# Gates of half the tokens by indirect transfers through a matrix in DRAM, in a four-layer decoder with product-key experts

## The chip, the cores and the metric

One core of one Trainium2 chip runs the whole program in one launch. The metric is the device time of an execution in microseconds (us), lower being better. TensorE is the engine of the matrix products (PE, its weight loads PEld), VectorE is DVE, ScalarE is ACT, GpSimd is POOL; SyncE (SP) issues most DMA transfers.

## The reference

256 tokens of width 1024 go through four layers. Each has a token mixer (sliding-window, dilated, latent, sliding-window), a normalisation, the product-key expert stage `peer`, and a second normalisation. `peer` takes most of the time:

```python
q = (t @ w_q).reshape(n_tok, 8, 2, 128)
sc = einsum('thpd,hpkd->thpk', q, keys)            # 8 heads x 2 halves x 128 keys
s_top, i_top = top_k(sc, 16)
cand = s_top[:, :, 0, :, None] + s_top[:, :, 1, None, :]
best, sel = top_k(cand.reshape(n_tok, 8, 256), 16) # 16 experts of 16384 for a head
idx  = (i_top[..0..] * 128 + i_top[..1..]) at sel
gate = softmax(best)
h = gelu(einsum('cd,ced->ce', t, u[idx]))          # 128 experts for a token
y = einsum('ce,ced->cd', gate * h, v[idx])
```

All data are float32. An expert that two heads of one token pick gets the sum of both gates.

## The kernel before, in words

The kernel gathers no rows of `u` and `v`. It multiplies all 256 tokens with all 16384 experts and zeroes what is not chosen: `G[expert, token] = gelu(t u) * gate`, and `y = G v`, where the gate is 0 for experts not chosen. A float32 product is made of three products of float32r parts (hi*hi, lo*hi, hi*lo): ACT makes `hi`, DVE or POOL makes `lo = raw - hi` (`_split`, L82).

All weights come as one list of 512 KB chunks (`plan`, L49), in the order of use. `nxt` (L98) hands out a chunk: it splits up to two chunks ahead (`SPLITAHEAD`), and SP loads up to three ahead of the splits (`RAWBUFS`). Every engine's order is the order of the Python calls.

`peer` (L892) has these stages for each layer:

- **Scores** (`peer_scores`, L720): 16 chunks of `w_q`, then products with the keys.
- **First products** (the loop over j at L928, 128 chunks of `u`): 24 matmuls of 256 columns (L121) give the scores of 128 experts for 256 tokens, ACT applies Gelu into `G`. `G[0]` holds the first 64 chunks, `G[1]` the rest.
- **Second products** (the loop at L969, 128 chunks of `v`): ACT and DVE split `G[j]` (L961, L962), and 12 matmuls of 512 columns (L131 to L135) add to `y`. The last five chunks go through `sum_norm`.

Under the first products a side generator runs on DVE, paced by a budget of estimated DVE microseconds for each chunk (`pace`, L708; each `yield` names a cost). It is first `topk_gen` (L744): the 16 best of 128 scores for each half of each head and both halves of the tokens, candidates, 16 best of those, their row and column among 128x128 experts, softmax; TensorE turns the table (L855). Then it is `weights_gen` (L859): for each unit of 4 tokens DVE builds two one-hot matrices (L869, L871; one carries the gate), and TensorE multiplies them into a 128x128 gate matrix for each token (L885), 64 units in all. `keep` (L904) brings that into `G`: for chunks whose Gelu comes later it is copied by ACT, and Gelu is multiplied in (`times`, L923); for chunks already there DVE multiplies (L917). `pool_share` says which part of the `lo` subtractions POOL takes.

## Time and profile before

| what | value |
|---|---|
| median of 3 runs | 3997.86 us (3997.18 to 3999.26) |
| profiled execution, own time | 4000.66 us |
| profiled execution, span on the core | 3998.8 us |
| TensorE busy | 98% of the span |
| VectorE, ScalarE, GpSimd busy | 75%, 47%, 8% |
| bytes moved | 668.00 MB, 167 GB/s in the mean |

The span runs from the first to the last instruction; the profiled execution's own time has 1.9 us more around it. Busy time is the union of an engine's instructions; since matmuls are pipelined, the distance from start to start tells more of their price than their duration.

### The profile page before, as it was taken

The numbers are of one execution on the slowest core, as the hardware profiler recorded it, in microseconds if no ns is written. First come the engines' busy times: TensorE is split into PE (matmuls) and PEld (weight loads), VectorE is DVE, ScalarE is ACT, GpSimd is POOL, SyncE is SP. The second block draws the span as 40 slices with busy tenths as digits, with TensorE's granted clock in tenths as the row PEclk, the third lists the DMA queues.
The fourth block names the chain that finished last, engine by engine and source line by source line (L and its number), as shares of the span: only waits on it lengthen the run. The fifth ranks groups of instructions, "written<-read, shape, count | busy, mean of one in ns | idle before, by whom it ended". The sixth has DMA issues, their size and how long they took to land. (4 is left out here: it accounts for less than half of the span.)

```text
span 3998.8 us, 68740 instructions
## 1 busy us (share of the span) xinstructions
PE 3934.8 (98%) x26592; PEld 3579.7 (90%) x26592; DVE 3017.9 (75%) x5798; ACT 1894.6 (47%) x3568; POOL 336.1 (8%) x135
## 2 busy tenths in 40 slices
PE   8999999999999999999999999999999999999999
PEld 6999998888998999988887999998888899998887
DVE  7888985566667989965557888985566788996555
ACT  5444444445554444444445444434445444444444
POOL 0111110000001111100000111110000111110000
PEclk9999999999999999999999999999999999999999
DMA  5454445564444554455653554445564455445554
GB/s 182 161 185 151 143 148 187 203 215 156 140 143 143 175 174 143 138 169 189 215 182 105 169 183 152 143 142 187 197 221 148 143 181 168 143 138 175 189 199 159
DMA packets 188007, 668.00 MB, mean 167 GB/s; under 512 B 20688, under 2 KB 27408, under 8 KB 187168
## 3 DMA queue, kind: packets, MB, share of 16 engines
q1 hardware_dynamic: 187424, 663.46, 49.8%
q8 instruction: 209, 3.42, 0.3%
q14 instruction: 118, 0.97, 0.1%
q0 software_dynamic: 64, 0.08, 0.0%
q10 hardware_dynamic: 192, 0.07, 0.0%
HBM read 662.46 MB, written 1.07 MB: 166 GB/s over the span
## 5 line engine op out<-in xcount | busy, mean ns | idle before, releaser
L94 DVE TENSOR_TENSOR lo<-raw,hi 128x1024 fp32r<-128x1024 f32 x1083 | 1324.3, 1223 | 825.4 <-ACT hi L88 821.7
L88 ACT ACTIVATE hi<-raw 128x1024 fp32r<-128x1024 f32 x1212 | 1281.3, 1058 | 724.6 <-PE y L135 696.3
L121 PE MATMUL hp<-zh,hi 128*128 128x256 f32 x5360 | 784.5, 289 | 2.5 <-ACT zh L222 1.7
L121 PE MATMUL hp<-zh,lo 128*128 128x256 f32 x5360 | 752.6, 283 | 0.0
L121 PE MATMUL hp<-zl,hi 128*128 128x256 f32 x5360 | 751.3, 283 | 0.0
L121 PEld LDWEIGHTS hp<-zh,hi 128*128 128x128 f32 x5360 | 689.4, 192 | 9.6 <-issue 4.5
L121 PEld LDWEIGHTS hp<-zh,lo 128*128 128x128 f32 x5360 | 691.7, 192 | 0.0
L121 PEld LDWEIGHTS hp<-zl,hi 128*128 128x128 f32 x5360 | 691.4, 192 | 0.0
L133 PE MATMUL y<-lo,wk 128*128 128x512 f32 x2004 | 632.5, 396 | 0.0
L131 PE MATMUL y<-hi,wk 128*128 128x512 f32 x2004 | 629.0, 394 | 3.5 <-ACT wk L961 3.3
L135 PE MATMUL y<-hi,wk 128*128 128x512 f32 x2004 | 631.8, 396 | 0.2 <-DVE wk L999 0.2
L94 POOL TENSOR_TENSOR lo<-raw,hi 128x1024 fp32r<-128x1024 f32 (+1 forms) x129 | 334.7, 2596 | 3293.6 <-ACT hi L88 3090.5
L131 PEld LDWEIGHTS y<-hi,wk 128*128 128x128 f32 x2004 | 375.7, 188 | 96.6 <-ACT wk L961 4.1
L135 PEld LDWEIGHTS y<-hi,wk 128*128 128x128 f32 x2004 | 376.0, 188 | 93.3 <-DVE wk L999 0.6
L133 PEld LDWEIGHTS y<-lo,wk 128*128 128x128 f32 x2004 | 376.2, 188 | 89.2
L941 ACT ACTIVATE gtmp<-hp 128x256 f32<-128x256 f32 (+52 forms) x284 | 80.6, 284 | 615.3 <-PE hp L121 313.6
L869 DVE TENSOR_TENSOR wk<-iota,tab 128x1024 f32<-128x1024 f32 x256 | 314.1, 1227 | 0.1
L885 PE MATMUL y<-wk 128*128 128x128 f32 x2048 | 271.1, 275 | 13.5 <-DVE wk L871 13.5
L885 PEld LDWEIGHTS y<-wk 128*128 128x128 f32 x2048 | 250.2, 192 | 15.7 <-DVE wk L871 15.7
L871 DVE TENSOR_TENSOR wk<-wk,tab 128x512 f32<-128x512 f32 x256 | 245.7, 960 | 8.8
L946 ACT ACTIVATE G<-hp 128x256 f32<-128x256 f32 x228 | 87.6, 384 | 340.9 <-PE hp L121 340.6
L962 DVE TENSOR_TENSOR wk<-G,wk 128x256 fp32r<-128x256 f32 x492 | 206.0, 419 | 2.4 <-ACT wk L961 2.4
(190 smaller groups left out, 2686.0 us busy)
## 6 DMA issues: line engine op xcount, KB each, us to landing
raw<-in_peer_u SPq DMA_DIRECT2D x512, 512.0 KB, 3.3
raw<-in_peer_v SPq DMA_DIRECT2D x512, 512.0 KB, 3.3
raw<-in_dil_w SPq DMA_DIRECT2D x72, 512.0 KB, 3.6
raw<-in_peer_wq SPq DMA_DIRECT2D x64, 512.0 KB, 3.6
raw<-in_swa_w SPq DMA_DIRECT2D x20, 512.0 KB, 4.0
G<-in_lnp SPq DMA_DIRECT2D x16, 512.0 KB, 4.6
raw<-in_swa_wo SPq DMA_DIRECT2D x16, 512.0 KB, 3.5
G<-relb SPq DMA_DIRECT2D x12, 512.0 KB, 4.7
```

Of the source, the lines that this page charges most:

```text
L88: nc.scalar.activation(h[:, :w], r[:, :w], AF.Copy)
L94: eng.tensor_sub(lo[:, :w], r[:, :w], h.bitcast(F32)[:, :w])
L121: mm(ps, w[:, k, :], z[:, k0 + k, :], start=(p == 0 and k == 0), stop=(p == 2 and k == nk - 1))
L131: mm(ps[t][b][:, :s.stop - s.start], zh[:, ts], hi[:, s], start=first, stop=False)
L133: mm(ps[t][b][:, :s.stop - s.start], zh[:, ts], lo[:, s], start=False, stop=False)
L135: mm(ps[t][b][:, :s.stop - s.start], zl[:, ts], hi[:, s], start=False, stop=last)
L869: V.tensor_tensor(ab, self.iota[:, None, None, :].to_broadcast(shape), tab[:, 0:2, ts][:, :, :, None].to_broadcast(shape), op=OP.is_equal)
L871: V.tensor_mul(ab[:, 1], ab[:, 1], tab[:, 2, ts][:, :, None].to_broadcast([128, 4, 128]))
L885: nc.tensor.matmul(p[:, k, :], ab[:, 0, k, :], ab[:, 1, k, :], start=True, stop=True)
L941: nc.scalar.activation(tmp[:, 0:td], ps[:, 0:td], AF.Gelu)
L946: nc.scalar.activation(g, ps, AF.Gelu)
L962: nc.vector.tensor_sub(gz[:, 1, :], g, gz.bitcast(F32)[:, 0, :])
```

## The change

The 256 tokens are treated in two halves.

- For tokens 0 to 127 no matrices are built by TensorE. A matrix of 128x128x128 floats (8 MB) in DRAM, `gates[i]`, one for each layer, is zeroed beforehand by 64 transfers of 128 KB on SP's queue (`next_gates`, `clear`). `topk_gen` now finishes this half of the tokens first, makes an element number for each of a token's 128 experts (`ids`, column * 16384 + row * 128 + token), and calls `ready`. That issues 128 indirect transfers on POOL's queue (`scatter`): each adds one float for each of the 128 tokens. The 16 transfers of a head may be in flight together; each head waits until the head before it has landed.
- In the second products, `gated(j)` multiplies `G[j]`'s first 128 columns by the gates, which SP fetches two chunks at a time (128 KB) into two buffers `gt`. The first fetch waits for all transfers of `scatter`.
- For tokens 128 to 255 everything stays, with 32 units in place of 64, from the last token down.
- The costs in the `yield`s and the budgets are changed (2.0 for a chunk until the first half is ready, then 1.6; before 1.3). POOL takes 40% of the `lo` subtractions until `ready` and none after it (before 20%). POOL's queue isn't tied to the program's order against the other engines any more.

```diff
+    def clear(self, n):
+        while n and self.to_clear:
+            n -= 1
+            self.nc.sync.dma_start(self.to_clear.pop(0), self.zero[:, None, :].to_broadcast([128, 2, 128]))
+    def next_gates(self, i):
+        self.clear(999)
+        self.gates.append(self.dram.tile([128 * 128 * 128, 1], F32, name=f"gates{i}"))
+        v = self.gates[-1].rearrange("(n p b c) o -> n p b (c o)", p=128, b=2, c=128)
+        self.to_clear = [v[k] for k in range(64)]
     def nxt(self, ahead=SPLITAHEAD):
         i = self.n_use
+        self.clear_acc += self.clear_rate
+        while self.clear_acc >= 1:
+            self.clear_acc -= 1
+            self.clear(1)
...
-            self.pace(1.3)
+            self.pace(2.0)
...
+            if t == 0:
+                V.tensor_scalar(row, row, 128.0, self.steps[:, 32:33], op0=OP.mult, op1=OP.add)
+                yield 0.28
+                V.scalar_tensor_tensor(col, col, 16384.0, row, op0=OP.mult, op1=OP.add)
+                yield 0.28
+                V.tensor_copy(ids, col)
+                yield 0.28
...
+            if t == 0:
+                ready()
...
-        for u in range(66):
-            if u + 1 < 64:
+        for u in range(34):
+            if u + 1 < 32:
                 build(u + 1)
...
+    def scatter(self, i, ids, val):
...
+        for h in range(8):
+            head = f"gates {i} {h}"
+            new = []
+            for k in range(16 * h, 16 * h + 16):
+                ins = self.nc.gpsimd.indirect_dma_start(
+                    self.gates[i], IndirectOffsetOnAxis(ap=ids[:, k:k + 1], axis=0), val[:, k:k + 1], None,
+                    compute_op=OP.add).ins
+                if new:
+                    tc.declare_no_dep(ins, group=head, reason="experts of one head differ")
+                self.all_done(ins, sent, "the same token's gates of another head")
...
+        def ready():
+            self.clear(999)
+            self.pool_share = 0.0
+            sent.extend(self.scatter(i, ids, val))
+
+        self.side = self.topk_gen(ids, val, tab, ready)
+        self.pool_share = 0.4
...
-                rate = 67.0 / (125 - j)
+                rate = 35.0 / (125 - j)
+            if j == 64 and i + 1 in self.layers:
+                self.next_gates(i + 1)
+                self.clear_rate = 0.5
...
+        rows = self.gates[i].rearrange("(n b p c) o -> n p b (c o)", b=2, p=128, c=128)
+        gts = []
+        def fetch(n):
+            while len(gts) < min(n, 64):
+                gt = self.misc.tile([128, 2, 128], F32, name="gt", bufs=2)
+                ins = nc.sync.dma_start(gt, rows[len(gts)]).ins
+                if not gts:
+                    self.all_done(ins, sent, "the gates are read")
+                gts.append(gt)
+        def gated(j):
+            if j < 128:
+                fetch(j // 2 + 2)
+                g = G[j // 64][:, j % 64, 0:128]
+                nc.vector.tensor_mul(g, g, gts[j // 2][:, j % 2, :])
...
         n = 128 - YTAIL
+        gated(0)
+        gated(1)
         z = split_g(0)
         for j in range(n):
+            gated(j + 2)
             hi, lo = self.nxt(min(SPLITAHEAD, n - 1 - j))
...
+            self.next_gates(self.layers[0])
+            self.clear_rate = 2.0
```

Three places of the order, all in the first layer. In the rows of the changed kernel, `L97` is the `lo` subtraction, `L81` the load of a chunk, `L929` the indirect transfer, `L1027` the fetch, `L1036` the multiplication by fetched gates, `L105` a clearing transfer, `L987` is `times`, `L1042` the split of `G`; names in brackets are what the instruction waits for (`DMAHW` and `DMASW` are transfers of SP's and of POOL's queue).

First, POOL's queue under the first products. Before, it holds only `lo` subtractions there. Now, after the 16th of them:

```order
L97 TENSOR_TENSOR lo<-raw,hi 128x1024 [waits DMAHW5_49,PE_49,Activation_49]
L929 DMA gates_140<-gt 2097152x1 [waits DMAHW7_49,DMAHW2_49,DVE_49]
L929 DMA gates_140<-gt 2097152x1 x5
L929 DMA gates_140<-gt 2097152x1 [waits DMASW0_49]
...
L929 DMA gates_140<-gt 2097152x1 [waits DMASW1_49]
L929 DMA gates_140<-gt 2097152x1 [waits DMASW4_49,DMASW5_49,DMASW3_49,DMASW6_49,DMASW2_49,DMASW7_49,DMASW1_49,DMASW0_49]
L929 DMA gates_140<-gt 2097152x1 x7
L929 DMA gates_140<-gt 2097152x1 [waits DMASW2_49]
```

Within a head's 16 transfers the later ones wait, one after another, for transfers issued eight before them; the first of the next head waits for all eight lanes. No subtraction stands among the 128 transfers.

Second, SP's queue at the change from first to second products. Before:

```order
L78 DMA raw<-in_peer_u 128x1024 [waits DMAHW5_49,DVE_49]
L78 DMA raw<-in_peer_v 128x1024 [waits DMAHW6_49,Pool_49]
L78 DMA raw<-in_peer_v 128x1024 [waits DMAHW7_49,DVE_49]
L78 DMA raw<-in_peer_v 128x1024 [waits DMAHW0_49,DVE_49]
L78 DMA raw<-in_peer_v 128x1024 [waits DMAHW1_49,DVE_49]
```

Now:

```order
L81 DMA raw<-in_peer_v 128x1024 [waits DMAHW6_49,DVE_49]
L81 DMA raw<-in_peer_v 128x1024 [waits DMAHW4_49,DMAHW0_49,DVE_49]
L1027 DMA gt<-gates_140 128x2x128 [waits DMASW4_49,DMASW5_49,DMASW3_49,DMASW6_49,DMASW2_49,DMASW7_49,DMASW1_49,DMASW0_49]
L1027 DMA gt<-gates_140 128x2x128
L1027 DMA gt<-gates_140 128x2x128 [waits DMAHW7_49,DMAHW5_49,DVE_49]
L105 DMA gates_4232<-zero 256x1x128
L81 DMA raw<-in_peer_v 128x1024 [waits DMAHW1_49,DVE_49]
```

The first fetch stands behind the load of the fifth chunk of `v`, waits for POOL's transfers, and all further loads stand behind it.

Third, DVE at the same place. Before:

```order
L94 TENSOR_TENSOR lo<-raw,hi 128x1024 [waits DVE_49,DMAHW2_49,PE_49,Activation_49]
L924 TENSOR_TENSOR G_3644<-G_3644,gtmp 128x256
L924 TENSOR_TENSOR G_3644<-G_3644,gtmp 128x256 [waits Activation_49]
L962 TENSOR_TENSOR wk<-G_1675,wk 128x256 [waits DVE_49,Activation_49]
L94 TENSOR_TENSOR lo<-raw,hi 128x1024 [waits DVE_49,DMAHW3_49,PE_49,Activation_49]
L962 TENSOR_TENSOR wk<-G_1675,wk 128x256 [waits Activation_49]
```

Now:

```order
L97 TENSOR_TENSOR lo<-raw,hi 128x1024 [waits DVE_49,DMAHW0_49,PE_49,Activation_49]
L987 TENSOR_TENSOR G_4003<-G_4003,gtmp 128x128
L987 TENSOR_TENSOR G_4003<-G_4003,gtmp 128x128 [waits Activation_49]
L1036 TENSOR_TENSOR G_1724<-G_1724,gt 128x128 [waits DMAHW5_49]
L1036 TENSOR_TENSOR G_1724<-G_1724,gt 128x128
L1042 TENSOR_TENSOR wk<-G_1724,wk 128x256 [waits Activation_49]
L1036 TENSOR_TENSOR G_1724<-G_1724,gt 128x128 [waits DMAHW6_49]
L97 TENSOR_TENSOR lo<-raw,hi 128x1024 [waits DMAHW1_49,PE_49,Activation_49]
```

A multiplication that waits for a fetch now stands ahead of each split of `G` and each `lo`. Counted along the queues, `ready` follows the 56th `lo` subtraction (40 on DVE and 16 on POOL); the subtractions run two chunks ahead of the products, and 34 chunks lie before the first products, so that is at chunk 19 of the 128.

## Rows read from the trace of the kernel before

**Rows 1.** The page's part 1: engine, busy us (share of the span), instructions.
```profile
PE 3934.8 (98%) x26592; PEld 3579.7 (90%) x26592; DVE 3017.9 (75%) x5798; ACT 1894.6 (47%) x3568; POOL 336.1 (8%) x135
```
**Rows 2.** Busy time of each engine in stretches of the first layer: the mixer, first products with the side generator on top-k, first products with units, second products, and the change to the next layer. Last: granted clock, share of the DMA engines, GB/s.
```profile
10.00:95.00 85.00, 76.30 (x535) 63.51 (x534) 69.82 (x203) 46.52 (x125) 4.88 (x2) 1.00 0.49 162
153.00:310.00 157.00, 157.00 (x1311) 157.00 (x1311) 132.99 (x377) 77.64 (x114) 28.68 (x11) 1.00 0.54 181
310.00:583.00 273.00, 269.75 (x2283) 269.14 (x2281) 259.18 (x380) 114.38 (x288) 37.52 (x14) 1.00 0.43 144
583.00:942.00 359.00, 358.93 (x1540) 288.80 (x1541) 217.39 (x277) 175.42 (x257) 0.39 (x1) 1.00 0.58 198
946.00:950.00 4.00, 3.02 (x19) 3.05 (x20) 3.38 (x5) 0.97 (x2) 0.28 (x1) 0.78 0.66 230
```
**Rows 3.** Timeline of PE, first products without units (start us, duration us): the first matmuls of one chunk and of the next (a chunk is three such groups of 8; the second row is cut by the window's end).
```profile
302.79 1.12 PE L121 MATMUL hp<-zh,hi 128*128 128x256 f32 x8
305.67 0.40 PE L121 MATMUL hp<-zh,hi 128*128 128x256 f32 x2
```
**Rows 4.** The same with units: a unit (four float32 matmuls, eight instructions) and the next one; one chunk lies between them (the last row is cut by the window's end).
```profile
318.71 1.05 PE L885 MATMUL y<-wk 128*128 128x128 f32 x8
322.48 0.38 PE L885 MATMUL y<-wk 128*128 128x128 f32 x2
```
**Rows 5.** Timeline of PE: the turning of the top-k table.
```profile
308.55 0.82 PE L855 MATMUL sm<-ident,G 128*128 128x128 f32 x6
```
**Rows 6.** The page's part 5: units on PE, the one-hot matrices and the `lo` subtraction on DVE (busy us, mean ns | idle before); and from the waits of PE: what units waited for (us in total, times, longest).
```profile
L885 PE MATMUL y<-wk 128*128 128x128 f32 x2048 | 271.1, 275 | 13.5 <-DVE wk L871 13.5
L869 DVE TENSOR_TENSOR wk<-iota,tab 128x1024 f32<-128x1024 f32 x256 | 314.1, 1227 | 0.1
L871 DVE TENSOR_TENSOR wk<-wk,tab 128x512 f32<-128x512 f32 x256 | 245.7, 960 | 8.8
L94 DVE TENSOR_TENSOR lo<-raw,hi 128x1024 fp32r<-128x1024 f32 x1083 | 1324.3, 1223 | 825.4 <-ACT hi L88 821.7
PE y L885 <- DVE wk L871: 13.5, 11, 1.7
```
**Rows 7.** DVE under the first products: two first instructions of one top-16 of 128 scores and of the next, with one `lo` subtraction between them (timeline); and the group of 128x128 float32 multiply-like instructions (by line, 150 to 310 us).
```profile
181.28 0.27 DVE L760 MAX8 G<-G 128x8 f32<-128x128 f32 x1
183.99 0.28 DVE L760 MAX8 G<-G 128x8 f32<-128x128 f32 x1
L823 DVE TENSOR_TENSOR G<-G 128x128 f32<-128x128 f32 x2 | 0.6, 292 | 0.1
```
**Rows 8.** POOL: its only transfers of 128 pieces are two plain loads, one shown (duration ns min/median/max); its `lo` subtractions; one of them in the timeline, and a conversion on DVE beside it.
```profile
L1098 POOL DMA_DIRECT2D iota<-in_iota x1: 540/540/540, 1.9 to 1.9; - x1
L94 POOL TENSOR_TENSOR lo<-raw,hi x129: 1807/2410/3402, 90.1 to 3628.3; 128x1024 fp32r<-128x1024 f32 x127, 128x768 fp32r<-128x768 f32 x2
192.13 3.18 POOL L94 TENSOR_TENSOR lo<-raw,hi 128x1024 fp32r<-128x1024 f32 x1 [11.99 <-ACT hi L88]
193.95 1.51 DVE L778 CAST G<-G 128x256 f32<-128x256 uint32 x1
```
**Rows 9.** DMA issues: what, queue, count, KB each, median us from issue to landing. A chunk comes in 128 pieces of 4 KB, `relb` in 512 pieces of 1 KB; `y` is written to DRAM.
```profile
raw<-in_peer_v SPq DMA_DIRECT2D x512, 512.0 KB, 3.3
G<-relb SPq DMA_DIRECT2D x12, 512.0 KB, 4.7
y<-x SPq DMA_DIRECT2D x4, 256.0 KB, 2.0
iota<-in_iota POOLq DMA_DIRECT2D x1, 64.0 KB, 5.2
```
**Rows 10.** The page's part 3: SP's queue: packets, MB, share of 16 engines' span.
```profile
q1 hardware_dynamic: 187424, 663.46, 49.8%
```
**Rows 11.** The change from first to second products in the first layer: DVE's `lo` of the chunk two ahead, the loads SP issues behind it (three, merged), PE's last group and its first of the second products, DVE's split of `G`.
```profile
580.82 1.23 DVE L94 TENSOR_TENSOR lo<-raw,hi 128x1024 fp32r<-128x1024 f32 x1 [1.32 <-ACT hi L88]
582.07 6.83 SPq L78 DMA_DIRECT2D raw<-in_peer_v  x3
581.12 1.12 PE L121 MATMUL hp<-zl,hi 128*128 128x256 f32 x8
583.07 0.73 PE L131 MATMUL y<-hi,wk 128*128 128x512 f32 x2 [0.83 <-ACT wk L961]
583.09 0.42 DVE L962 TENSOR_TENSOR wk<-G,wk 128x256 fp32r<-128x256 f32 x1
```
**Rows 12.** Timeline of PE at the change of layers: an idle time, and the matmuls after it.
```profile
946.98 2.61 PE L217 MATMUL sm<-gtmp,x 128*128 128x128 f32 x16 [2.57 <-DVE x L180]
949.24 2.25 PE L121 MATMUL hp<-zh,hi 128*128 128x256 f32 x8
951.29 1.28 PE L121 MATMUL hp<-zh,lo 128*128 128x256 f32 x8
```
**Rows 13.** Timeline of DVE in the second products: `lo`, split of `G`, the next `lo`.
```profile
702.07 1.23 DVE L94 TENSOR_TENSOR lo<-raw,hi 128x1024 fp32r<-128x1024 f32 x1 [1.24 <-ACT hi L88]
703.21 0.42 DVE L962 TENSOR_TENSOR wk<-G,wk 128x256 fp32r<-128x256 f32 x1
704.87 1.23 DVE L94 TENSOR_TENSOR lo<-raw,hi 128x1024 fp32r<-128x1024 f32 x1 [1.24 <-ACT hi L88]
```

More of the change, by code (lines that the diff above doesn't have):

```diff
@@ L8 @@
 from concourse import mybir
+from concourse.bass import IndirectOffsetOnAxis
 from concourse.bass_utils import run_bass_kernel_spmd
@@ L39 @@
 YTAIL = 5
+ET = mybir.EngineType
+ORDERED = {ET.PE, ET.DVE, ET.Activation, ET.SP}
 class Kernel:
@@ L837, in topk_gen @@
-        V.tensor_copy(den[:, 0, :][:, :, None], b3[:, :, 0:1])
-        V.tensor_sub(b3, b3, den[:, 0, :][:, :, None].to_broadcast([128, 16, 16]))
-        yield 0.2
-        nc.scalar.activation(best, best, AF.Exp)
-        yield 0.2
-        V.tensor_reduce(den[:, 1, :], b3, axis=AX.X, op=OP.add)
-        yield 0.2
-        V.reciprocal(den[:, 2, :], den[:, 1, :])
-        yield 0.2
-        for t in range(2):
-            V.tensor_mul(stk[:, t, 2, :].rearrange("p (h k) -> p h k", h=8), best[:, t],
-                         den[:, 2, 8 * t:8 * t + 8][:, :, None].to_broadcast([128, 8, 16]))
-            yield 0.2
+                yield 0.7
@@ new lines, in topk_gen @@
+                V.tensor_reduce(col[:, ks].rearrange("p (h k) -> p h k", h=4), ohb, axis=AX.X, op=OP.add)
+                yield 1.23
+            V.tensor_copy(row, idi[:, 1, :])
+            yield 0.28
+            if t == 0:
+                V.tensor_scalar(row, row, 128.0, self.steps[:, 32:33], op0=OP.mult, op1=OP.add)
+                yield 0.28
+                V.scalar_tensor_tensor(col, col, 16384.0, row, op0=OP.mult, op1=OP.add)
+                yield 0.28
+                V.tensor_copy(ids, col)
+                yield 0.28
@@ new lines, in topk_gen @@
+            V.tensor_copy(den[:, 0, :][:, :, None], best[:, :, 0:1])
+            V.tensor_sub(best, best, den[:, 0, :][:, :, None].to_broadcast([128, 8, 16]))
+            yield 0.5
+            nc.scalar.activation(best, best, AF.Exp)
+            yield 0.2
+            V.tensor_reduce(den[:, 1, :], best, axis=AX.X, op=OP.add)
+            yield 0.28
+            V.reciprocal(den[:, 2, :], den[:, 1, :])
+            yield 0.2
+            V.tensor_mul((stk[:, 2, :] if t else val).rearrange("p (h k) -> p h k", h=8), best,
+                         den[:, 2, :][:, :, None].to_broadcast([128, 8, 16]))
@@ L850, in topk_gen @@
+            yield 0.28
+            if t == 0:
+                ready()
         yield 0
         yield 0
-        for t in range(2):
-            p = self.small((128, 4, 128))
-            for q in range(3):
-                nc.tensor.transpose(p[:, q, :], stk[:, t, q, :], self.ident)
-            V.tensor_copy(tab[:, 0:3, t * 128:t * 128 + 128], p[:, 0:3, :])
-            yield 0.2
+        p = self.small((128, 4, 128))
+        for q in range(3):
+            nc.tensor.transpose(p[:, q, :], stk[:, q, :], self.ident)
@@ L859, in weights_gen @@
+        V.tensor_copy(tab, p[:, 0:3, :])
+        yield 0.55
     def weights_gen(self, tab, keep):
@@ L887, in weights_gen, with all_done @@
                 due()
-            due = keep(4 * u - 4, kept.rearrange("p t j -> p j t")) if kept is not None else None
+            due = keep(256 - 4 * u, kept.rearrange("p t j -> p j t")) if kept is not None else None
             kept = p
             yield 1
+    def scatter(self, i, ids, val):
+        tc = self.tc
+        sent = []
+        for h in range(8):
[8 more added lines that the diff above has]
+                self.all_done(ins, sent, "the same token's gates of another head")
+                tc.add_to_no_dep_group(head, ins)
+                new.append(ins)
+            sent = new
+        return sent
+    def all_done(self, ins, sent, reason):
+        for old in sent:
+            self.tc.add_manual_dep(ins, old.name, mybir.DependencyInfo(
+                mybir.DependencyClass.Sync, mybir.DependencyReason.DATA), reason=reason)
     def peer(self, i, turn):
@@ L996, in peer @@
                 gh, gl = [self.misc.tile([128, 1, T], F32R, name="gtmp", bufs=2) for _ in range(2)]
+            for q in range(m if k else 0):
+                gated(n + k + q)
             g = G[1][:, 64 - YTAIL + k:64 - YTAIL + k + m, :]
```

113 lines of the change are left out of this document (54 added, 59 removed).

## The prediction, made before the changed kernel ran

> **What bounds the kernel now.** I read the page's shares first: TensorE is busy for 98% of the span, VectorE for 75%, GpSimd for 8% [rows 1]. Then the stretches of one layer: under the first products TensorE is busy for 157.00 of 157 us and, with units, 269.75 of 273; in the second products for 358.93 of 359, and the granted clock is 1.00 (2.4 GHz) in all three [rows 2]. So every stage of `peer` ends with TensorE, and only what shortens its list shortens the time, as long as nothing else becomes later than it. The engine to watch is DVE: with units it is busy for 259.18 of 273 us [rows 2]. The DMA engines are at 0.43 to 0.58.
>
> **What is removed from TensorE.** A chunk of first products without a unit takes 305.67 - 302.79 = 2.88 us [rows 3]; with one unit, from unit to unit, 322.48 - 318.71 = 3.77 us [rows 4]. A unit so costs 0.89 us. (Its group in the page says 271.1 us for 256 units [rows 6]; that union of pipelined spans is 1.06 each, and the start-to-start distance is what the path gives back.) 32 units fewer in 4 layers are 128 x 0.89 = 113.9 us. Three of the six turns of the table go too, half of 0.82 us [rows 5], in 4 layers 1.6 us. Together **-115.5**.
>
> Units waited 13.5 us for their one-hot matrices [rows 6]. DVE then has one unit (1227 + 960 ns [rows 6]) for about every second chunk instead of for every one; I take back 5 us of the 13.5, since waits at the first units can stay; ends 0 and 13.5.
>
> **What stays hidden on DVE.** Each of 128 chunks needs one `lo` of 1.22 us [rows 6], which POOL takes no part of after `ready`. Top-k for the second half has a budget of 1.6 for a chunk. A top-16 of 128 scores takes 183.99 - 181.28 = 2.71 us with one `lo` among it [rows 7], so about 1.5 without, and the new `yield`s count 1.77 for it: a budget of 1.6 is about 1.4 us of work. 1.4 + 1.22 = 2.6 of 2.88 us: below TensorE, with a tenth to spare. With units at about 0.5 for a chunk DVE has 1.1 + 1.22 and some 0.5 for the multiplications into `G`, 2.8 of 3.3 us. In the second products it has 1.23 + 0.42 us for each 2.80 us [rows 13] and gets a 128x128 multiplication of 0.29 [rows 7]: 1.94. All this costs nothing.
>
> **The scatter.** It has from chunk 19 of the first products to their end: 108 chunks x 2.88 + 32 units x 0.89 = 340 us. It needs 8 heads x (16 c + L), where c is POOL's time for one indirect transfer and L the landing of a head's last. No row shows an indirect transfer. Low ends: the plain POOL load of 128 pieces, 0.54 us [rows 8], and the landing of the only larger DRAM write, 2.0 us [rows 9]: 8 x (8.6 + 2.0) = 85 us. High ends: the longest POOL instruction that reads SBUF beside a busy DVE, 3.40 us [rows 8], and POOL's own landing, 5.2 us [rows 9]: 8 x (54.4 + 5.2) = 477 us, 137 us late in each layer. I take c = 1.2, about twice the plain load, because that row is the nearest (POOL writes 128 pieces in both, and here also reads 128 numbers and asks for an addition), and L = 3.3: 8 x (19.2 + 3.3) = **180 us of 340**, so it costs nothing. It becomes late from c = 2.45.
>
> The DMA engines must carry it too: 16384 pieces of 4 bytes for each layer, 1024 for an engine. With about half of 340 us free [rows 2], a piece may hold an engine for 170/1024 = 0.17 us. A mean packet of 3.5 KB holds one for 0.498 x 16 x 3998.8/187424 = 0.17 us [rows 10], and I take a piece of 4 bytes to be cheaper.
>
> **Clearing and fetching.** 64 + 64 transfers of 128 KB for each layer, in 256 pieces of 512 bytes. 512 KB in 512 pieces land in 4.7 us against 3.3 in 128 pieces [rows 9]; 24 more pieces on each engine for 1.4 us, at most 0.058 us a piece, so a transfer of 256 pieces takes at most 0.93 us of the engines. By bytes alone it would be a quarter of a chunk's, under 0.5. In the second products a fetch comes every two chunks, in their first half a clearing transfer too: at most 0.17 + 0.17 on top of 0.58 [rows 2]. That is 0.92, still under 1. A fetch is issued behind the load that follows one `lo`, and its data are wanted two chunks and a split later, 2 x 2.80 + 0.42 = 6.0 us; it lands after 3.3 to 4.7 us. So in the steady state it costs nothing. In the first layer's mixer two clearing transfers stand ahead of each load; the engines are at 0.49 there [rows 2], TensorE is idle for 9 of 85 us already, and I add 3 us (0 to 15).
>
> **The new wait.** At the change to the second products the first fetch stands on SP behind the load that waits for DVE's `lo`: 582.07 in this trace [rows 11]. Issued 0.33 us later and landing after 3.3 us plus some 0.5 behind a full chunk, it is there at 586.2. Then `gated(0)` (0.29 us), ACT's split (about 0.4) and the handovers: TensorE starts at 587.1 instead of 583.07 [rows 11], 4.0 us later. Behind that wait on SP stand the next loads, and on DVE the split of `G` and the next `lo`; two further chunks are split already, so nobody but TensorE feels it. An idle time of 2.57 us was followed by eight matmuls in 2.05 us that otherwise take 0.96, and the granted clock is 0.78 in that stretch [rows 2, 12]; I add 1.5 us for it. 5.5 us x 4 = **+22**. With landings of 2.0 and 5.2 us the ends are +9 and +29.
>
> One more Exp for each layer (and its table) goes to ACT, busy for 114 of 273 us [rows 2]: nothing.
>
> **Sum.** -115.5 - 5 + 22 + 3 = -95.5 us, from the profiled execution's 4000.66 to 3905.2. That execution stands 2.8 us above the median of the runs, so **3902 us** is my time. The ends of the unknown terms make its own range 3875 to 3924.
>
> **The rivals.**
> - *The scatter comes late, and the kernel is slower.* POOL's queue becomes the bound: SP's first fetch waits for the last head, and all loads of `v` stand behind it, four times in a run. For it: a POOL subtraction of median 2.41 us took 3.18 while DVE ran a conversion, which took 1.51 us itself [rows 8], and DVE is over 90% busy; waiting for landings of earlier transfers adds to c. Against it: 0.54 us for the plain load. It decides from c = 2.64 on, where 8 x (42.2 + 3.3) = 364 us is 24 us late in each layer and the gain is gone. At c = 3.4 it is 137 us late: +548 - 95 gives some 4450; at c = 2.9 and L = 4, 403 us, 63 late, 4154. The Trainium skill, *SBUF — State Buffer*, section "A bandwidth-pool intuition that's wrong (but worth ruling out)", says that a transfer prepared by GpSimd that takes about 620 ns alone takes about 3100 beside a VectorE copy, because GpSimd can't write its descriptors while VectorE holds the shared port; with that figure the chain would be an estimated 423 us and the time 4234. The trace agrees as far as the two stretched instructions go, but most of DVE's work after `ready` isn't copies.
> - *Late by less than the gain* (c of 2.45 to 2.64, or pieces that hold the engines for about 0.17 us): 3902 to 3990.
> - *The gain is eaten elsewhere.* If DVE's instructions wait for POOL's, half a transfer (0.6 us) for each `lo`, DVE needs 3.2 of 2.88 us for the 62 chunks of the scatter: 0.35 x 62 x 4 = 87 us, 3989. Or pieces of 512 bytes cost 0.1 us and not 0.058: the first half of the second products needs 0.58 + 2 x 0.29 = 1.16 of the engines, 64 x 2.8 x 0.16 x 3 layers = 86 us, 3988. Both together with the other slips end within 0.2% of before.
> - *The change doesn't do what it says*, for instance because POOL's order puts subtractions among the transfers: in the order none stands there, so I give it nothing.
>
> **How the numbers follow.** Forecast 0.62, partly late 0.07, eaten elsewhere 0.08 (0.05 of it within 0.2%), late and slower 0.23. What a measurement of this kernel can tell from no change is about 0.2%, 8 us. Faster: 0.62 + 0.07 + 0.03 = 0.72; the same 0.05; slower 0.23. The range begins at the forecast's low end, 3875, and reaches up over the eaten gains into the smaller lateness, to 4090 (c of about 2.8); some 0.06 lies below it and 0.14 above.
>
> **What would show it.** Right: 1024 unit matmuls on PE at the same spacing; POOL's 128 transfers start at chunk 19 and end about 180 us later, well ahead of the second products; PE idle for about 5 us at each change to them; raised DMA shares of at most 0.9. Wrong: PE idle for tens of us there, with SP waiting for POOL's queue; `lo` late under the first products; or second products at over 2.80 us for a chunk.

## The result, and the profile after

The changed kernel takes **3881.69 us** (median of 4, 3877.22 to 3884.34); the kernel before takes 3997.97 beside it. The ratio is 0.9708 [0.9691, 0.9725]: 116 us, where 96 were forecast. The profiled execution took 3882.64 us, its span is 3880.9.

From the page: busy time of the engines, SP's and POOL's queues, and the groups that answer to [rows 1, 6, 10] (busy us, mean ns | idle before). In the changed kernel `L141` is the matmuls of the first products, `L151` to `L155` those of the second, and `L1041` ACT's part of the split of `G`.

```profile
PE 3808.2 (98%) x25556; PEld 3473.0 (89%) x25556; DVE 2789.0 (72%) x5885; ACT 1880.9 (48%) x3420; POOL 1195.5 (31%) x589
...
q1 hardware_dynamic: 326688, 730.60, 58.0%
q0 software_dynamic: 73792, 0.38, 5.2%
...
L97 DVE TENSOR_TENSOR lo<-raw,hi 128x1024 fp32r<-128x1024 f32 x1141 | 1399.1, 1226 | 930.5 <-ACT hi L91 928.1
L929 POOL DMA_INDIRECT gates<-gt x512 | 1016.2, 1985 | 265.3 <-issue 188.4
L1036 DVE TENSOR_TENSOR G<-G,gt 128x128 f32<-128x128 f32 x512 | 145.7, 286 | 15.3 <-DMA gt<-gates 15.2
```

TensorE still fills 98% of a shorter span. POOL goes from 8 to 31%, and 1016.2 of its 1195.5 us are 512 indirect transfers of 1985 ns. The forecast had set 1.2 us for one.

The same stretches as in [rows 2], where the first products now end at 555.4 us and the second ones begin at 559.7; the three short ones lie at that change.

```profile
10.00:95.00 85.00, 78.14 (x529) 65.21 (x528) 69.46 (x204) 46.61 (x125) 4.65 (x2) 0.99 0.69 218
153.00:310.00 157.00, 154.10 (x1272) 153.90 (x1272) 141.17 (x400) 75.24 (x110) 97.63 (x41) 0.99 0.61 178
310.00:555.00 245.00, 245.00 (x2063) 245.00 (x2063) 179.83 (x278) 112.48 (x250) 178.56 (x96) 1.00 0.72 179
555.00:560.00 5.00, 0.69 (x5) 0.49 (x4) 1.51 (x6) 1.19 (x4) 0.00 (x0) 0.81 0.48 159
560.00:562.50 2.50, 2.50 (x7) 1.92 (x8) 2.09 (x5) 0.92 (x2) 0.00 (x0) 0.50 0.36 105
562.50:565.00 2.50, 2.50 (x8) 1.95 (x7) 0.00 (x0) 0.00 (x0) 0.00 (x0) 0.51 0.65 210
570.00:915.00 345.00, 343.86 (x1501) 281.45 (x1500) 236.73 (x393) 170.47 (x249) 0.00 (x0) 1.00 0.74 237
```

With units TensorE now lacks nothing (245.00 of 245), and DVE is down to 179.83 of 245. The fetches and clearings raise the DMA share in the second products from 0.58 to 0.74; TensorE stays busy for 343.86 of 345 us there. At the change to the second products the granted clock is 0.50 for five microseconds: the lower of its two levels, 1.2 GHz.

The waits of PE (us in total, times, longest):

```profile
PE y L151 <- ACT wk L1041: 18.0, 4, 4.7
...
PE hp L141 <- DVE lo L97: 6.1, 3, 2.9
...
PE y L151 <- ACT wk L1083: 4.9, 4, 1.3
```

The units' 13.5 us are gone. The new entry costs 18.0 us in four times (3.3 before), a `lo` under top-k comes late three times, and the last five chunks wait for their split. All three lie ahead of their layer's scatter. In the longest (2.9 us, at 212.01) a DVE operation with two inputs that starts at 207.77, 0.4 us into a `lo` on POOL of 2.38 us, takes 3.05 us where the same operation took 1.22 at 204.53.

The first of these in the timeline, in the order of PE, SP and DVE, answers to [rows 11]:

```profile
559.72 1.22 PE L151 MATMUL y<-hi,wk 128*128 128x512 f32 x2 [4.31 <-ACT wk L1041]
560.74 1.05 PE L153 MATMUL y<-lo,wk 128*128 128x512 f32 x2
...
555.88 3.93 SPq L1027 DMA_DIRECT2D gt<-gates  x3
...
558.93 0.49 DVE L1036 TENSOR_TENSOR G<-G,gt 128x128 f32<-128x128 f32 x2 [2.71 <-DMA gt<-gates]
559.70 0.43 DVE L1042 TENSOR_TENSOR wk<-G,wk 128x256 fp32r<-128x256 f32 x1 [0.28 <-ACT wk L1041]
```

The fetch is issued at 555.88, DVE can multiply by its data from 558.93, ACT splits, TensorE starts at 559.72. Its first matmuls then stand 427 ns apart instead of some 230, eight to eleven of them in each layer: the first chunk takes 4.8 to 5.3 us instead of 2.9.

Stage by stage, summed over the four layers of the two profiled executions (start of first matmul to start of first matmul; "first products" without the idle time at their end):

| part | before | after | change | forecast |
|---|---|---|---|---|
| first products with units | 1722.9 | 1598.6 | -124.3 | -120.5 |
| idle time at the entry to the second products | 3.3 | 18.0 | +14.7 | +16 |
| second products and what follows them | 1443.8 | 1438.4 | -5.4 | +6 |
| mixers, scores, start | 828.8 | 825.9 | -2.9 | +3 |
| sum | 3998.8 | 3880.9 | -117.9 | -95.5 |

The second products should have become 9 us longer by their half-clock chunks alone, yet they are shorter. A chunk in them takes 2.80 us before in all layers; after, in the profiled execution, 2.747 in three layers and 2.80 in the fourth. Nothing in the forecast spoke of that: 3 x 123 x 0.053 = 19.5 us. The experiments had to settle two things: what made an indirect transfer dear, and how near that came to the path; and where the rhythm came from.

### The profile page after: what moved, and what is told of

It is laid out like the page before. It is cut to its first block, busy times and chain, and to the rows that moved or that the text cites. A ratio compares the mean times of both kernels' runs of the same rounds, so it can differ in the third digit from the quotient of the medians.

```text
span 3880.9 us, 68042 instructions
## 1 busy us (share of the span) xinstructions
PE 3808.2 (98%) x25556; PEld 3473.0 (89%) x25556; DVE 2789.0 (72%) x5885; ACT 1880.9 (48%) x3420; POOL 1195.5 (31%) x589
## 3 DMA queue, kind: packets, MB, share of 16 engines
q0 software_dynamic: 73792, 0.38, 5.2%
q14 instruction: 130, 1.06, 0.1%
## 4 chain that ended last, share of the span: by engine, by line
PE 92%; DVE 5%; ACT 1%; DMA 1%; issue 1%; SPq 0%; ACTq 0%; DVEq 0%
PE hp L141 48%; PE y L151 13%; PE y L153 12%; PE y L155 12%; PE y L913 3%; DVE lo L97 1%; PE sm L751 1%; PE sm L321 1%; PE y L355 0%; ACT hi L91 0%; DVE x L206 0%; DMA raw<-in_swa_w 0%; PE sm L237 0%; DVE x L200 0%; DVE G L328 0%
## 5 line engine op out<-in xcount | busy, mean ns | idle before, releaser
L97 DVE TENSOR_TENSOR lo<-raw,hi 128x1024 fp32r<-128x1024 f32 x1141 | 1399.1, 1226 | 930.5 <-ACT hi L91 928.1
L929 POOL DMA_INDIRECT gates<-gt x512 | 1016.2, 1985 | 265.3 <-issue 188.4
L97 POOL TENSOR_TENSOR lo<-raw,hi 128x1024 fp32r<-128x1024 f32 (+1 forms) x71 | 177.7, 2507 | 2020.9 <-ACT hi L91 2020.9
L141 PE MATMUL hp<-zh,hi 128*128 128x256 f32 x5360 | 773.7, 287 | 2.5 <-ACT zh L242 1.7
L141 PE MATMUL hp<-zh,lo 128*128 128x256 f32 x5360 | 753.6, 283 | 6.1 <-DVE lo L97 6.1
L141 PE MATMUL hp<-zl,hi 128*128 128x256 f32 x5360 | 753.1, 283 | 0.0
L141 PEld LDWEIGHTS hp<-zh,hi 128*128 128x128 f32 x5360 | 689.9, 192 | 9.8 <-issue 4.5
L141 PEld LDWEIGHTS hp<-zh,lo 128*128 128x128 f32 x5360 | 692.2, 192 | 6.7 <-DVE lo L97 6.7
L141 PEld LDWEIGHTS hp<-zl,hi 128*128 128x128 f32 x5360 | 692.2, 192 | 0.0
L151 PE MATMUL y<-hi,wk 128*128 128x512 f32 x2004 | 629.3, 395 | 23.0 <-ACT wk L1041 18.0
L155 PE MATMUL y<-hi,wk 128*128 128x512 f32 x2004 | 627.5, 394 | 0.0
L1001 ACT ACTIVATE G<-hp 128x256 f32<-128x256 f32 (+28 forms) x512 | 181.8, 355 | 838.6 <-PE hp L141 838.4
L151 PEld LDWEIGHTS y<-hi,wk 128*128 128x128 f32 x2004 | 378.6, 189 | 108.5 <-ACT wk L1041 18.9
L155 PEld LDWEIGHTS y<-hi,wk 128*128 128x128 f32 x2004 | 378.8, 189 | 86.8 <-DVE wk L1042 0.4
L1042 DVE TENSOR_TENSOR wk<-G,wk 128x256 fp32r<-128x256 f32 x492 | 206.5, 420 | 2.7 <-ACT wk L1041 2.7
L1041 ACT ACTIVATE wk<-G 128x256 fp32r<-128x256 f32 x492 | 197.1, 401 | 20.0 <-DVE G L1036 14.2
L416 ACT ACTIVATE G<-hp 128x256 f32<-128x256 f32 x156 | 59.6, 382 | 207.5 <-PE hp L141 204.8
L1036 DVE TENSOR_TENSOR G<-G,gt 128x128 f32<-128x128 f32 x512 | 145.7, 286 | 15.3 <-DMA gt<-gates 15.2
L897 DVE TENSOR_TENSOR wk<-iota,tab 128x1024 f32<-128x1024 f32 x128 | 156.1, 1219 | 0.0
```

Of the source, the lines that this page charges most:

```text
L97: eng.tensor_sub(lo[:, :w], r[:, :w], h.bitcast(F32)[:, :w])
L141: mm(ps, w[:, k, :], z[:, k0 + k, :], start=(p == 0 and k == 0), stop=(p == 2 and k == nk - 1))
L151: mm(ps[t][b][:, :s.stop - s.start], zh[:, ts], hi[:, s], start=first, stop=False)
L155: mm(ps[t][b][:, :s.stop - s.start], zl[:, ts], hi[:, s], start=False, stop=last)
L897: V.tensor_tensor(ab, self.iota[:, None, None, :].to_broadcast(shape), tab[:, 0:2, ts][:, :, :, None].to_broadcast(shape), op=OP.is_equal)
L929: ins = self.nc.gpsimd.indirect_dma_start(self.gates[i], IndirectOffsetOnAxis(ap=ids[:, k:k + 1], axis=0), val[:, k:k + 1], None, compute_ ...
```

## The experiments

Where a kernel leaves work out, its expectation says so. "Chunk" below is the mean distance of chunks in the second products.

**units_only** does the change's gain without its price: no scatter, clearing, fetch or gating.

```diff
-            sent.extend(self.scatter(i, ids, val))
-            if j < 128:
+            if False:
                 fetch(j // 2 + 2)
```

> One part alone: half of the units are gone, and nothing takes their place. There is no matrix in DRAM, no clearing, no indirect transfer, no fetch and no multiplication by fetched gates; the gates of tokens 0 to 127 are left out of G, which is what this kernel doesn't compute. Theory (what is removed from TensorE comes back in full, and the rest costs only at the entry to the second products): no wait there beyond the 0.8 us of before, full clock, 2.80 us for a chunk of second products as before, so 3997.9 - 113.9 - 1.6 - 13.5 = 3869 us (3863 to 3875). Rival (DMA traffic or GpSimd's transfers slow the products all along): the removed part alone is worth much more than the whole change kept, below 3850. Rival (units are worth less than start-to-start distances say): above 3880.

Measured: 3852.02 us (3845.75 to 3854.37), 0.9637 [0.9622, 0.9651]. The idle time at the entry is 0.84 us as before, and yet the chunk is 2.747 us in all four layers: 4 x 123 x 0.053 = 26 us that the expectation did not have. The profiled execution, the fastest of the four, is lower by about that; the median is 17 us below the 3869 expected, outside the range of the theory and of both rivals. What quickens the second products is neither the fetch nor the lower clock.

**no_scatter** drops only the 128 indirect transfers (the gates fetched are zeros).

```diff
-            sent.extend(self.scatter(i, ids, val))
```

> The change without its 128 indirect transfers for each layer: clearing, fetching and multiplying stay, so tokens 0 to 127 get gates of 0, which is what this kernel leaves out. Theory (the scatter is hidden, it ended 17 to 25 us ahead of the fetch): the same as the change, 3877 to 3885, with an idle time of 4 to 5 us at each entry to the second products as before; at most 6 us less where a lo subtraction waited at the start of the scatter. Rival (the scatter costs time on the path though it ends early, through DVE or the DMA engines): below 3870.

Measured: 3886.82 us (3877.54 to 3890.89), 0.9714 [0.9699, 0.9729]: 5 us above the change and 2 above the range expected, but the ranges of the two overlap; entry idle 17.8 us, fourth layer at 2.80. The scatter itself costs nothing on the path. The waits for a `lo` (8.2 us) are there without it, so it isn't their cause.

**early_fetch** keeps everything, but issues the first fetches in chunk 125 of the first products, and the first gating and split in chunk 126.

```diff
+            if j == 125:
+                fetch(2)
+            if j == 126:
+                gated(0)
+                gated(1)
+                z = split_g(0)
...
-        gated(0)
-        gated(1)
-        z = split_g(0)
```

> The whole change, but the first two fetches are issued under chunk 125 of the first products, and the first two multiplications and the first split of G under chunk 126. Theory (the wait at the entry is the fetch's landing): TensorE's idle time there falls from 4.5 us to about 0 and the clock stays at its upper level, 4 x (4.5 + 2.4) = 28 us. How the second products then run is open: if entering them at the lower clock is what made a chunk take 2.75 us in three layers, they go back to 2.80 and give 19 us away: about 3873. If 2.75 belongs to the change itself (another layout of the on-chip memory, another traffic), about 3854. Rival (the entry isn't on the path): 3882.

Measured: 3854.69 us (3849.14 to 3857.16), 0.9639 [0.9626, 0.9653]. The timeline of PE shows no idle time and no lower clock at the entry:

```profile
554.49 1.12 PE L141 MATMUL hp<-zl,hi 128*128 128x256 f32 x8
555.45 0.62 PE L151 MATMUL y<-hi,wk 128*128 128x512 f32 x2
555.91 0.39 PE L153 MATMUL y<-lo,wk 128*128 128x512 f32 x1
```

It is 27 us below the change: 18 of idle time, 9 of half clock and the fourth layer's 6.5 are saved, and some 6 are given back (3 of them in the first products). Its median also stands 3 us above that of units_only, which does none of the new work and still has 3.4 us of idle time at its entries: scatter, clearing, fetching and gating cost some 6 us once the entry is mended.

**early_both** also multiplies the last five chunks by their gates under the chunks before them, so that their splits needn't wait.

```diff
-            gated(j + 2)
+            upto(j + 3 + max(0, j - (n - 4)))
...
-            for q in range(m if k else 0):
-                gated(n + k + q)
```

> As early_fetch, and the multiplications of the last five chunks are done under the chunks before them, so that ACT's split of the last chunks doesn't wait for them. Theory: another 4 x 1.2 = 5 us below early_fetch, and the last chunks at the period of the others. Rival (those waits are hidden by two chunks of lead): the same as early_fetch.

Measured: 3860.89 us (3858.53 to 3863.28), 6 us slower than early_fetch where 5 less were expected. The wait for ACT's split falls from 5.7 to 3.8 us, and 2.6 us for DVE's split take its place. That is 0.7 us more; where the rest of the 6 comes from isn't shown.

**before_early** asks whether the entry without idle time chooses the rhythm, in the kernel before.

```diff
+            if j == 126:
+                self.pace(9999)
+                z = split_g(0)
...
-        z = split_g(0)
```

> The kernel before with one edit: the first split of the second products (its activation and its subtraction) is issued in chunk 126 of the first products, ahead of their end, so that TensorE should go from the last first product to the first second product without the idle time of 0.83 us. Nothing else moves; all 256 tokens stay with TensorE's units. Theory (the rhythm of the second products is one of two steady states of TensorE and is chosen by how it enters them; without idle it enters the quick one, as in all four layers of early_fetch): mean chunk 2.747 instead of 2.80 us in all four layers, 4 x 123 x 0.053 = 26 us, and with the 3.3 us of idle time saved 3998 - 26 - 3 = 3968 us (3963 to 3974). Rival (the units, the addresses of the tiles or the other work of the kernel before set the slower rhythm): chunk 2.80, only the idle time saved, 3994 us (3992 to 3998).

Measured: 3994.12 us (10 runs, 3991.88 to 3996.03), 0.9991 [0.9981, 1.0]: the rival's number. The chunk stays at 2.80 in all layers.

**before_entry_wait** puts the change's wait into the kernel before.

```diff
+        gt = self.misc.tile([128, 2, 128], F32, name="gt", bufs=1)
+        nc.sync.dma_start(gt, self.a["masks"][:, 0:256].rearrange("p (b c) -> p b c", b=2))
+        g0 = G[0][:, 0, 0:128]
+        nc.vector.scalar_tensor_tensor(g0, gt[:, 0, :], 0.0, g0, op0=OP.mult, op1=OP.add)
         z = split_g(0)
```

> The kernel before with one edit: ahead of the first split a transfer of 128 KB is issued and an operation of VectorE that reads it and leaves the gates as they were, so that TensorE waits there some 4 to 5 us in each layer as in the change. Theory (the entry chooses the rhythm, and an entry at half clock mostly falls into the quick one: three layers of four in the change): idle time 3.5 to 4 us more per layer and 1.5 to 2.4 us for matmuls at the lower clock, 4 x 5.5 to 6 = 22 to 24 us more, and 6.4 us less for each layer that turns quick: three of four give 3998 + 23 - 19 = 4002 us (3996 to 4016). Rival (something else of the kernel before sets its rhythm): chunk 2.80 in all layers, 4021 us (4018 to 4026).

Measured: 4024.04 us (4022.98 to 4024.9), 1.0066 [1.005, 1.0083], again the rival's. Its waits of PE:

```profile
PE y L131 <- ACT wk L961: 19.1, 4, 5.6
```

It has 15.8 us more of idle time, and its first chunks take 7.3 us more in the sum of the four layers. That is 23 of the 26 us between the medians; the two profiled executions are 22.4 apart. The chunk stays at 2.80. So the price of the entry is confirmed, and the second theory of the rhythm has fallen too.

**lo_on_act** asks what makes an indirect transfer dear. In the change, under top-k, POOL and DVE run like this (timeline of each):

```profile
237.31 2.58 POOL L929 DMA_INDIRECT gates<-gt  x1 [0.30 <-issue]
240.19 2.58 POOL L929 DMA_INDIRECT gates<-gt  x1 [0.30 <-issue]
243.07 2.58 POOL L929 DMA_INDIRECT gates<-gt  x1 [0.30 <-issue]
...
237.24 1.23 DVE L97 TENSOR_TENSOR lo<-raw,hi 128x1024 fp32r<-128x1024 f32 x1 [0.34 <-ACT hi L91]
...
240.12 1.23 DVE L97 TENSOR_TENSOR lo<-raw,hi 128x1024 fp32r<-128x1024 f32 x1
...
243.00 1.23 DVE L97 TENSOR_TENSOR lo<-raw,hi 128x1024 fp32r<-128x1024 f32 x1 [0.40 <-ACT hi L91]
```

Each transfer starts 0.07 us after a `lo` and takes 2.58 us; with 0.30 us to the next that is 2.88, just one chunk. POOL is locked to DVE's subtraction.

```diff
-        eng.tensor_sub(lo[:, :w], r[:, :w], h.bitcast(F32)[:, :w])
+        if self.lo_act:
+            nc.scalar.activation(lo[:, :w], r[:, :w], AF.Copy)
+        else:
+            eng.tensor_sub(lo[:, :w], r[:, :w], h.bitcast(F32)[:, :w])
```

> The change with one edit: in chunks 20 to 55 of the first products the low half of the weights is written by ScalarE as a plain copy, so that VectorE's operation with two inputs from SBUF is gone there (this leaves out the subtraction in those chunks). It asks what makes an indirect transfer take 2.58 us and keeps it at one per chunk. Theory (it waits for VectorE's two-input operation of 1.13 us that starts beside it): from chunk 20 on the transfers stand about 1.55 + 0.30 = 1.85 us apart, and the scatter ends some 80 to 100 us earlier in each layer. Rival (the descriptors, the landing of the one before or any VectorE work keep them): spacing stays at 2.3 us or more. The kernel's time: within 1% of the change by both, ScalarE having 1.1 us more per chunk there.

Measured: in that stretch, with the top-k work beside them as before, the transfers take 1.55 us and stand 1.86 apart. The timeline of POOL, without the `lo` and, further down, where DVE has them again:

```profile
240.27 1.55 POOL L932 DMA_INDIRECT gates<-gt  x1 [0.30 <-issue]
242.13 1.55 POOL L932 DMA_INDIRECT gates<-gt  x1 [0.30 <-issue]
243.98 1.55 POOL L932 DMA_INDIRECT gates<-gt  x1 [0.30 <-issue]
...
329.29 2.28 POOL L932 DMA_INDIRECT gates<-gt  x1 [0.30 <-issue]
331.88 2.43 POOL L932 DMA_INDIRECT gates<-gt  x1 [0.30 <-issue]
```

The one at 331.88 started 0.2 us into a one-hot comparison of DVE, also with two inputs, of 1.22 us. The theory holds in kind: DVE's long operations with two inputs from SBUF hold the transfer up, the short top-k operations on one input do not. Nor is it their length: in the change itself, a transfer that starts 0.1 us into a reduction of DVE on one input of 1.21 us takes 1.55 (POOL, then DVE):

```profile
304.72 1.55 POOL L929 DMA_INDIRECT gates<-gt  x1 [0.30 <-issue]
...
304.62 1.21 DVE L834 TENSOR_REDUCE G<-G 128x64 f32<-128x1024 f32 x1
```

The scatter takes 24 to 29 us less, not the 80 to 100 expected, since the stretch holds only two to three of the eight heads. The Trainium skill, *SBUF — State Buffer*, section "Who interferes with whom", says that a VectorE instruction with two SBUF inputs contends with a GpSimd instruction that reads SBUF. The trace agrees: 2.58 us is 1.55 and 1.03 more, nearly what is left of the `lo` when the transfer starts (1.16). The time, 3881.82 us (one run), is the change's: hidden is hidden.

**ten_heads** makes the scatter longer by two heads that add zeros.

```diff
-        for h in range(8):
-            head = f"gates {i} {h}"
+        for r in range(10):
+            h, val = (r, val) if r < 8 else (r - 8, self.zero)
+            head = f"gates {i} {r}"
```

> The change with one edit: after the eight heads two more rounds of 16 indirect transfers each add zeros to the first two heads' places, so the output stays and the scatter has 160 transfers instead of 128. Theory (the scatter runs beside the first products with only 23 to 25 us to spare, and TensorE waits for its end as soon as that is used up): two heads take 2 x 38 = 76 us, each layer enters its second products some 76 - 24 = 52 us later, 3882 + 4 x 52 = 4090 us (4040 to 4105). Rival (the fetch does not depend on the end of the scatter in this way, or the transfers go faster where the top-k work is over): 3882 us, or up to 3900.

Measured: 4059.9 us (one run). The timeline of POOL, SP and PE at the first layer's entry:

```profile
595.39 1.55 POOL L930 DMA_INDIRECT gates<-zero,gt  x1 [0.30 <-issue]
...
598.54 3.08 SPq L1028 DMA_DIRECT2D gt<-gates  x3
...
601.53 1.22 PE L151 MATMUL y<-hi,wk 128*128 128x512 f32 x2 [48.46 <-ACT wk L1042]
```

Each layer waits 48 to 50 us, 45 more than in the change: 179 us in all, against a measured difference of 178. The last two heads cost 34 to 37 and 29 us instead of 38 each, 63 to 66 together: the last runs behind the first products, where DVE has no long operation left, and its transfers take 1.55 us. The time is 30 us below the 4090 expected, within its range. The rival "the scatter comes late" is thus real, and the change is within one head of it.

**before_moved, after_moved, early_moved64, before_moved96.** What units_only and the change share, and the kernel before lacks, is the place of the tiles in SBUF. `wk`, which holds the split gates, is TensorE's stationary operand in `proj_n`; it begins at byte 214304 of each partition before, and at 214848 in the change, since ahead of it in the pool `zero` is new and `steps` is one column wider. In the kernel before, `wk` is the only tile behind `steps` that these chunks touch; in the change `gt` lies there too. One number moves them:

```diff
-        self.steps = self.misc.tile([128, 32], F32, name="steps", bufs=1)
-        nc.gpsimd.dma_start(self.steps, a["steps"])
+        self.steps = self.misc.tile([128, 40], F32, name="steps", bufs=1)
+        nc.gpsimd.dma_start(self.steps[:, 0:32], a["steps"])
```

> The kernel before with one number changed: the tile steps is 40 columns wide instead of 32, of which 32 are used. It stands ahead of the tile wk (the split gates, TensorE's stationary operand of the second products) in the same pool, so wk moves by 32 bytes, from byte 214304 of each partition (a multiple of 32 but not of 64) to 214336 (a multiple of 64), as it has one in the change (214848). No instruction differs otherwise. Theory (where the stationary tile begins sets the rhythm of the second products): mean chunk 2.747 instead of 2.80 us in all or nearly all layers, 4 x 123 x 0.053 = 26 us less, 3998 - 26 = 3972 us (3968 to 3985). Rival (the units or the program around them set it): 2.80 and 3998 us.

> The changed kernel with the same kind of edit the other way: steps is 41 columns wide instead of 33, so wk moves by 32 bytes from 214848 (a multiple of 64) to 214880 (not one), as in the kernel before. Theory (place of the stationary tile): mean chunk 2.80 us in all layers instead of in one of four, 3 x 123 x 0.053 = 19 to 20 us more, 3882 + 20 = 3902 us (3898 to 3906). Rival (the change's other work sets it): three layers at 2.747, 3882 us (3877 to 3891).

> early_fetch with steps 49 columns wide instead of 33: wk moves by 64 bytes, from 214848 to 214912, and stays at a multiple of 64 (now also of 128). Theory (a multiple of 64 is what counts): chunk 2.747 us and 3855 us as early_fetch (3849 to 3858). Rival (any other place changes the rhythm, or larger multiples give a third one): a chunk other than 2.747 us, and a time off by 123 x 4 times the difference.

> The kernel before with steps 56 columns wide instead of 32: wk moves by 96 bytes, from 214304 to 214400, a multiple of 128. Theory (the place of the stationary tile sets the rhythm, and a multiple of 128 gives the 2.72 us of early_moved64 in any of these kernels): 4 x 123 x 0.080 = 39 us less than before, 3959 us (3955 to 3966). Rival (2.72 us is particular to early_moved64, through its program or its entry without idle time): 2.747 us and 3972 us, as in before_moved, or 2.80 us and 3998 us.

| kernel | `wk` begins at | modulo 128 | chunk, us | time, us | ratio to before |
|---|---|---|---|---|---|
| before | 214304 | 32 | 2.80 in 4 layers | 3997.2 | 1 |
| before_moved | 214336 | 64 | 2.747 in 4 | 3971.82 (3969.68 to 3974.65) | 0.9936 [0.9919, 0.9952] |
| before_moved96 | 214400 | 0 | 2.72 in 4 | 3960.29 (3958.58 to 3961.71) | 0.9906 [0.9889, 0.9922] |
| the change | 214848 | 64 | 2.747 in 3, 2.80 in 1 | 3881.69 | 0.9708 [0.9691, 0.9725] |
| after_moved | 214880 | 96 | 2.80 in 4 | 3905.38 (3899.74 to 3908.03) | 0.9765 [0.9749, 0.9781] |
| early_fetch | 214848 | 64 | 2.747 to 2.752 in 4 | 3854.69 | 0.9639 [0.9626, 0.9653] |
| early_moved64 | 214912 | 0 | 2.72 to 2.726 in 4 | 3844.07 (3841.94 to 3847.02) | 0.9618 [0.9602, 0.9634] |

The profile shows it as the count of matmuls in 300 us of second products (windows; the second number after the stretch is PE's busy time, with its instructions in brackets): the kernel before, before_moved and before_moved96 from 600 us on; the change, after_moved and early_moved64 from 580 us on; and last the change in its fourth layer.

```profile
600.00:900.00 300.00, 300.00 (x1287) 241.37 (x1286) 180.73 (x227) 146.40 (x215) 0.00 (x0) 1.00 0.59 202
```
```profile
600.00:900.00 300.00, 300.00 (x1312) 246.19 (x1311) 183.96 (x230) 149.42 (x219) 0.00 (x0) 1.00 0.61 205
```
```profile
600.00:900.00 300.00, 300.00 (x1326) 248.39 (x1325) 185.29 (x232) 151.12 (x222) 0.00 (x0) 1.00 0.62 207
```
```profile
580.00:880.00 300.00, 300.00 (x1312) 245.96 (x1311) 205.55 (x340) 149.08 (x219) 0.00 (x0) 1.00 0.76 243
```
```profile
580.00:880.00 300.00, 300.00 (x1287) 240.97 (x1286) 201.60 (x334) 146.16 (x214) 0.00 (x0) 1.00 0.75 239
```
```profile
580.00:880.00 300.00, 300.00 (x1323) 247.54 (x1322) 207.02 (x344) 150.34 (x221) 0.00 (x0) 1.00 0.77 245
```
```profile
3550.00:3850.00 300.00, 300.00 (x1288) 242.99 (x1287) 188.95 (x322) 146.16 (x214) 0.00 (x0) 1.00 0.65 215
```

TensorE is "busy" for 300.00 of 300 us in every row, at a clock of 1.00, and does 1287 to 1326 matmuls in that time. Busy time can't show such a loss; counts, or distances from start to start, do. What follows: the place of `wk` sets the rhythm, in both directions, in kernels with and without the change. That the place acts through TensorE's load of the stationary operand is argued from its being that operand, not shown. The theory of early_moved64, that a multiple of 64 is enough, failed: a multiple of 128 gives a third rhythm. The fourth layer of the change at 2.80 us, though `wk` is at a multiple of 64, stays open: no_scatter has the same, lo_on_act and ten_heads have 2.747 there. Of the kernels that leave nothing out early_moved64 is the quickest, 153 us below the kernel before.

## Why the prediction came out as it did

It said 3902 us within 3875 to 4090; 3881.69 came. It was right in its main line; one of its terms was badly mis-sized without harm, and one thing that it took as fixed moved.

- **Units, turns, unit waits.** Forecast -113.9, -1.6 and -5; the first products give -124.3. The upper end of the third term was the right one: all 13.5 us of unit waits went, and 6.1 us of waits for a `lo` came (one of the prediction's signs of being wrong, but small), so -113.9 - 1.6 - 13.5 + 6.1 = -122.9. The price of 0.89 us for a unit, from start to start, holds; the page's 1.06 would have given 22 us more.
- **DVE under top-k.** Forecast 2.6 of 2.88 us; it was busy for 141.17 of 157 us, 2.59 for a chunk, and TensorE waited for it three times. A `lo` took 1226 ns in the mean against 1223 before [rows 6], so the rival that DVE waits for POOL's transfers didn't come.
- **The scatter: the step that failed.** c was set at 1.2 us "because that row is the nearest", the plain POOL load. It was 1.985 + 0.30 = 2.29: 1.55 for POOL alone, 0.30 between two transfers, and 0.43 in the mean of waiting for DVE, which the late rival had named as its mechanism (for copies; what the runs show is the operations with two inputs, and copies were not tested). The first layer's chain took 315 us instead of 180, from the first of these transfers to the end of the last:

```profile
217.96 1.66 POOL L929 DMA_INDIRECT gates<-gt  x1 [8.22 <-DVE G L782]
...
531.31 1.63 POOL L929 DMA_INDIRECT gates<-gt  x1 [0.30 <-issue]
```

The fetch went out at 555.9, 23 us after that end and some 21 after the landing (in ten_heads, where the fetch does wait for the scatter, it is issued 1.6 us after the last transfer ends). The window (340 us, measured 338), the landing of a head (3.3 us; the next head starts 3.3 us later in the mean) and the bound (late from c = 2.45) were right, and 2.29 is just under it. That a term of nearly twice its size did no harm is luck: ten_heads shows that some 64 us more would have taken the kernel past the one before. A chance of 0.30 for the late cases was not too much. The transfers' load on the DMA engines was sized rightly as small: a packet of POOL's queue held one for 0.052 x 16 x 3880.9/73792 = 0.044 us in the mean, where 0.17 would have been too much.

- **Clearing and fetching.** Forecast at most 0.92 of the DMA engines; 0.74 to 0.76. TensorE waited for it nowhere but at the entry, and the 3 us for the first mixer didn't come. The rival "eaten elsewhere" was added up wrongly: DVE's waits and dearer pieces together are 87 + 86 = 173 us, which gives 4075; only each alone ends near the time of before.
- **The new wait.** Forecast 4.0 us of idle time and 1.5 for the clock in each layer, +22; the idle time grew by 3.7, and the first chunk by 2.2. The half clock was under-estimated: eight matmuls of 256 columns had lost 1.1 us [rows 12], here eight to eleven of 512 columns stand 427 ns apart. The waits of the last chunks, 4.9 us, weren't thought of.
- **The second products' rhythm: not thought of.** A chunk of 2.80 us was taken as fixed. The change moved `wk` by 544 bytes and made three layers quicker, -19.5 us. With `wk` at a multiple of 32 only, as before, the change stands at 3905.38, 92 us below the kernel before: -95.5 was forecast. That the two agree so closely is partly luck: by the table, without the 19.5 us, the terms missed by -3.8, -1.3, +8.1 and -5.9 us, which nearly cancel. (The ends of the terms as stated give an own range of 3878 to 3926, not 3875 to 3924.) So some 92 us are the change's own, and some 24 are a gift of the pool's layout that one number in the kernel before would have brought as well (25 us in before_moved).

## What to carry to other kernels

Price a moved step by the queue it goes to and by what runs beside it (an indirect transfer took 1.55 us alone and 2.58 behind a two-input VectorE operation), and say how much of its window is left. When an engine that is always busy gets quicker or slower without a visible reason, count its instructions in a fixed time and look where its operands lie: a change that adds or shrinks a tile moves its neighbours, and two kernels compare fairly only with those places equal. Put the first fetch and split of a stage ahead of the end of the stage before it: that brought 27 us here.

## What the runs showed of the hardware

- float32 matmuls of 512 columns at 2.4 GHz with a new stationary operand each run in one of three steady rhythms: 233.3, 229 or 226.7 ns from start to start (2.80, 2.747, 2.72 us for twelve). Seen with the stationary tile at 32 or 96, at 64, and at 0 bytes modulo 128; in the second case 233.3 in single layers too.
- An idle time of TensorE of 4.3 to 4.7 us (the change's four entries) is followed by eight to eleven matmuls of 512 columns at 427 ns, granted clock 0.50 in the first layer; after an idle time of 0.84 us (units_only) the clock stays at 1.00.
- An indirect transfer of 128 single floats with addition takes POOL 1.55 us with 0.30 us between two of them. It takes up to 2.60 us when it starts during a VectorE operation with two inputs from SBUF, and still 1.55 during a reduction of 1.21 us on one.
- The other way round, a VectorE operation with two inputs that takes 1.22 us took 3.05 when it started 0.4 us into a two-input subtraction of GpSimd.
